# Two-layer hybrid diffusion block on one Trainium2 core: turned queries written into the free half of their own tile, neighbourhood queries staged two to a tile, squares of four heads in one instruction, and another order of VectorE and TensorE where each norm begins

## The chip, the cores and the metric

The kernel runs on one core of a Trainium2 chip. The metric is the device time of one execution, in microseconds (us), on that core; lower is better. The times of the kernel before are the median and the spread of three runs. One more execution was recorded by the hardware profiler; all durations below come from it.

## The reference, cut to what matters

256 latent tokens of width 2048, with 256 context tokens beside them in layer 0, pass through two layers. Layer 0 mixes with eight heads of a bidirectional gated DeltaNet and eight heads of neighbourhood attention; layer 1 mixes with a short gated convolution. Each layer ends with a SwiGLU network of 5632 hidden units. Everything is float32.

```python
for l in range(DEPTH):                                   # DEPTH = 2
    sh1, sc1, g1, sh2, sc2, g2 = split(silu(c) @ ada_w[l] + ada_b[l], 6)
    h = modulate(x_lat, norm_mix[l], sh1, sc1)           # rmsnorm * gain * (1 + sc) + sh
    y = even_mixer(h, hc, ...) if l == 0 else shortconv_mixer(h, ...)
    x_lat = x_lat + g1 * y
    x_lat = x_lat + g2 * swiglu(modulate(x_lat, norm_ffn[l], sh2, sc2), ...)
return rmsnorm(x_lat, final_norm)

def even_mixer(h, hc, w_in, ...):
    ka, va, kb, vb, a, b, qa, qb, za = split_segments(h @ w_in, EVEN_SEGS)
    ka, va, qa = short_conv_silu([ka, va, qa], conv_w)   # 5 taps along the tokens
    k_l = axial_rope(l2norm(heads(ka)))                  # l2norm: x * rsqrt(sum(x*x) + eps)
    q_l = axial_rope(l2norm(heads(qa))) * HEAD_DIM ** -0.5
    o_l, _ = gdn_bidirectional(q_l, k_l, heads(va), ...) # solve, inverse, scan over chunks of 64
    y_na = neighbourhood_attention(heads(qb), heads(kb), heads(vb), ...)
    return concat(y_gdn, y_na) @ w_out
```

## The kernel before

**Products.** Each float32 operand is split into a high and a low part, and each product is made of three matmuls: high by high, high by low, low by high. A weight arrives as a block of 512 KB, `raw` (128 partitions x 1024 float32), which SP loads (`load_w`, L232); `split_w` makes `whi` on ScalarE (a copy to fp32r, L175) and `wlo` on VectorE (a subtraction, L246). A block is a step of a stream (of the two forms below) where the stream is 1024 columns wide, and two steps where it is 512 wide.

**Streams.** `tm_stream` gives results with tokens on the partitions: per step, token tile (128 tokens, of which there are two) and block of 512 columns three matmuls, L299, L300 and L304. It keeps the last four steps for the end: there it takes block by block, each with four steps of three matmuls (L316), and after a block's twelve matmuls calls its evacuation. `fm_stream` gives results with features on the partitions, three matmuls (L342) per step and group of 128 features, and calls its evacuation for each group of 128 features on the last step. `grouped` collects the steps; behind a norm, the first HEAD = 4 steps are also done together, token tile by token tile. `Pump` runs the jobs of the conditioning product (`ada_w`, `araw`) between the steps.

**The end of a stream that a norm follows.** Three streams have such an end, each of two blocks on two token tiles: the mixer's output product (`ev_w_out`) ahead of layer 0's FFN, that FFN's down product ahead of the odd mixer, and the odd mixer's output (`od_w_out`) ahead of layer 1's FFN. `resid_evac` multiplies a block by the gate row (L1299), adds it to `xs`, the residual (L1300), and takes the sum of squares (L1301, ScalarE). After the first token tile's last block, `Lead.scale` makes the norm's factor of that tile and multiplies the first 512 columns by it (L1317). `Lead.turn` puts the four transposes (L194) of these 512 columns into TensorE's order, between the matmuls of the second tile's last block. `Norm.step` then takes a piece of 512 columns of one token tile: scale and shift from PSUM to `modt` (L1363, ScalarE), the cast to the high part (L1365 for the first piece, four casts of 128 columns, so that the first matmul can start early; L1367 for later ones), and the low part (L1368). `w_steps` makes the splits of the steps HEAD and HEAD + 1 (the fifth and sixth) of the next stream follow the last `modt` and the last `xc` (L1353) of the second tile's first piece; this pair of instructions is `Norm.behind`.

**The mixer.** Its stream of input products runs beside the DeltaNet chain: solves by DMA over DRAM (`zsol`, `lsol`, `dz`, `xd`), inverses, scans. Where each piece of that chain is placed between the stream's matmuls is a plan of step numbers (`P_INV = (30, 32, 82, 84)` for the inverses); within that the scheduler of the tile framework, which simulates the engines' times, sets the order of each engine, and of SP's DMA queue. A change of one instruction's cost or buffer can so change the order of all that follows.

- `head_evac` (L661) takes keys, values and queries of four heads. Four copies to `hst`, and then, deferred from step to step, `front` (`conv_silu`: the taps into a tile `cv`, of which there are CV = 4) and `back` (transposes into PSUM and a copy into `out_t`, a tile of 128 x 4 x 4 x 128: token tile, head, width). For keys (n = 4 token tiles) and queries (n = 2) the squares are summed on ScalarE, one instruction for each token tile and head (L687).
- `qa_evac` (L735) scales and rotates the queries in `qt` (that `out_t`; with n = 2 its last two of four quarters are empty), transposes two heads at a time, copies them to `qf` (another use of the four tiles `cv`) and sends them to DRAM with a DMA on SP (`qTd`).
- `stage` (L1170) copies the results of the neighbourhood attention's queries (256 columns, scaled), keys and values to a tile `nst` of 512 columns, of which there are three, and sends each with a DMA of its own on SP (`qb_d`, `kb_d`, `vb_d`, L1178).

The lines that matter most for the norm, as they stand before:

```python
                            if lead and ti and n == nb - 1 and g == 2:
                                before = lead.turn(ins)
...
                if not n:
                    DVE.tensor_copy(hi[:, k, tok], m[:, j, :])
            if n:
                DVE.tensor_copy(hi[:, ks_, tok], m)
            DVE.tensor_tensor(lo[:, ks_, tok], m, hi[:, ks_, tok], op=OP.subtract)
            if not n and t:
                self.behind = mi, xi
```

## Time and profile before

| what | value |
|---|---|
| median of three runs | 2759.35 us |
| the runs | 2752.03, 2759.35, 2764.47 us |
| the profiled execution | 2762.49 us |
| its span in the trace | 2760.7 us |
| busy: TensorE (PE) | 2663.2 us |
| busy: weight loads (PEld) | 2187.7 us |
| busy: VectorE (DVE) | 1908.4 us |
| busy: ScalarE (ACT) | 1284.3 us |
| mean granted clock of TensorE | 0.992 |
| weight splits on VectorE (L246), 800 | 969.0 us, 1221 ns each |
| weight copies on ScalarE (L175), 800 | 842.5 us, 1062 ns each |

The span is what the trace covers; the execution's own time has 1.8 us more around it. Busy times of different engines lie beside each other, so they don't add up to the span. TensorE's matmuls are pipelined: the length of one row of several is the time to the end of the last, and the pitch between two is less than the length of one. The granted clock is the share of full speed that the throttle gave TensorE. A row of the timeline has the start in us, the length in us, engine, line, operation and tiles, and in brackets the idle time of that engine just before it and who ended it.

### The profile page before, as it was taken

The numbers are of one execution on the slowest core, as the hardware profiler recorded it, in microseconds if no ns is written. First come the engines' busy times: TensorE is split into PE (matmuls) and PEld (weight loads), VectorE is DVE, ScalarE is ACT, GpSimd is POOL, SyncE is SP. The second block draws the span as 40 slices with busy tenths as digits, with TensorE's granted clock in tenths as the row PEclk, the third lists the DMA queues.
The fourth block names the chain that finished last, engine by engine and source line by source line (L and its number), as shares of the span: only waits on it lengthen the run. The fifth ranks groups of instructions, "written<-read, shape, count | busy, mean of one in ns | idle before, by whom it ended". The sixth has DMA issues, their size and how long they took to land.

```text
span 2760.7 us, 37649 instructions
## 1 busy us (share of the span) xinstructions
PE 2663.2 (96%) x13775; PEld 2187.7 (79%) x13775; DVE 1908.4 (69%) x2599; ACT 1284.3 (47%) x1923; POOL 52.5 (2%) x84
## 2 busy tenths in 40 slices
PE   5998999998989999999999999999999999999998
PEld 2588787886878788887888878887878888888886
DVE  2377787795768788777686668898678544445665
ACT  3267643333554544444455545444454444445554
POOL 0000000101000000000000000000000000000000
PEclk9999999999999999999999999999999999999999
DMA  9955478799747799998886548998569666656553
GB/s 345 329 180 162 138 240 286 230 316 285 227 182 263 264 335 328 352 324 309 276 297 193 194 148 323 321 329 290 190 230 334 222 195 186 190 186 222 192 193 114
DMA packets 287028, 684.81 MB, mean 248 GB/s; under 512 B 57209, under 2 KB 100833, under 8 KB 285307
## 3 DMA queue, kind: packets, MB, share of 16 engines
q1 hardware_dynamic: 280564, 669.26, 72.3%
q10 hardware_dynamic: 4375, 9.48, 1.0%
q0 software_dynamic: 1904, 3.67, 0.4%
q8 instruction: 108, 1.77, 0.2%
q14 instruction: 77, 0.63, 0.1%
HBM read 659.21 MB, written 23.10 MB: 247 GB/s over the span
## 4 chain that ended last, share of the span: by engine, by line
PE 74%; DMA 11%; DVE 7%; issue 3%; ACT 3%; SPq 2%; POOL 0%; DVEq 0%; ACTq 0%
PE mm L299 18%; PE mm L300 18%; PE mm L304 18%; PE mm L342 8%; DMA araw<-in_ada_w_dram 7%; PE mm L316 6%; DVE wlo L246 2%; PE sm L194 2%; DVE acc L396 2%; PE sm L574 1%; PE gd L342 1%; DVE acc L431 1%; DMA bq<-in_ev_rpb_dram 1%; DMA raw<-in_ev_w_in_dram 1%; ACT whi L175 1%
## 5 line engine op out<-in xcount | busy, mean ns | idle before, releaser
L246 DVE TENSOR_TENSOR wlo<-raw,whi 128x1024 fp32r<-128x1024 f32 x800 | 969.0, 1221 | 402.2 <-ACT whi L175 392.8
L175 ACT ACTIVATE whi<-raw 128x1024 fp32r<-128x1024 f32 x800 | 842.5, 1062 | 858.4 <-PE mm L304 618.5
L299 PE MATMUL mm<-whi,fhi 128*128 128x512 f32 x1232 | 484.5, 395 | 6.7 <-DVE fhi L1365 6.7
L300 PE MATMUL mm<-wlo,fhi 128*128 128x512 f32 x1232 | 481.7, 391 | 0.0
L304 PE MATMUL mm<-whi,flo 128*128 128x512 f32 x1232 | 389.9, 390 | 0.0
L396 DVE SCALAR_TENSOR_TENSOR acc<-araw,cT,acc 128x1024 f32<-128x1024 f32 x224 | 287.1, 1282 | 123.1 <-DMA araw<-in_ada_w_dram 116.2
L342 PE MATMUL mm<-hB,whi 128*128 128x512 f32 (+1 forms) x1064 | 276.9, 351 | 1.5 <-DVE hB L602 1.2
L299 PEld LDWEIGHTS mm<-whi,fhi 128*128 128x128 f32 x1232 | 232.5, 189 | 55.3 <-DVE fhi L1365 8.1
L300 PEld LDWEIGHTS mm<-wlo,fhi 128*128 128x128 f32 x1232 | 232.6, 189 | 47.0
L304 PEld LDWEIGHTS mm<-whi,flo 128*128 128x128 f32 x1232 | 231.1, 188 | 48.4
L299 PE MATMUL mm<-whi,ahi 128*128 128x512 f32 x664 | 259.0, 390 | 0.0
L300 PE MATMUL mm<-wlo,ahi 128*128 128x512 f32 x664 | 258.3, 389 | 0.0
L342 PEld LDWEIGHTS mm<-hB,whi 128*128 128x128 f32 x1064 | 183.5, 192 | 33.6 <-issue 4.2
L304 PE MATMUL mm<-whi,alo 128*128 128x512 f32 x664 | 206.7, 389 | 0.0
L342 PE MATMUL mm<-hB,wlo 128*128 128x512 f32 (+1 forms) x532 | 179.7, 351 | 0.0
L431 DVE SCALAR_TENSOR_TENSOR acc<-araw,cT,acc 128x512 f32<-128x512 f32 x192 | 142.6, 747 | 24.2 <-DMA araw<-in_ada_w_dram 19.9
L178 ACT ACTIVATE ahi<-prodT 128x256 fp32r<-128x256 f32 x176 | 73.0, 418 | 183.7 <-PE mm L300 182.3
L304 PEld LDWEIGHTS mm<-whi,alo 128*128 128x128 f32 x664 | 124.6, 188 | 25.9
L299 PEld LDWEIGHTS mm<-whi,ahi 128*128 128x128 f32 x664 | 124.6, 188 | 25.7
L300 PEld LDWEIGHTS mm<-wlo,ahi 128*128 128x128 f32 x664 | 124.7, 188 | 25.7
L299 PE MATMUL mm<-whi,dhi 128*128 128x512 f32 x336 | 132.3, 396 | 5.6 <-DVE dhi L1365 3.4
L300 PE MATMUL mm<-wlo,dhi 128*128 128x512 f32 x336 | 131.8, 393 | 0.0
(399 smaller groups left out, 3409.7 us busy)
## 6 DMA issues: line engine op xcount, KB each, us to landing
araw<-in_ada_w_dram SPq DMA_DIRECT2D x288, 512.0 KB
raw<-in_ffn_w_down_dram SPq DMA_DIRECT2D x176, 512.0 KB
raw<-in_ffn_w_gate_dram SPq DMA_DIRECT2D x160, 512.0 KB
raw<-in_ffn_w_up_dram SPq DMA_DIRECT2D x160, 512.0 KB
raw<-in_ev_w_in_dram SPq DMA_DIRECT2D x112, 512.0 KB
araw<-in_ada_w_dram SPq DMA_DIRECT2D x192, 256.0 KB
raw<-in_od_w_in_dram SPq DMA_DIRECT2D x96, 512.0 KB
raw<-in_ev_w_out_dram SPq DMA_DIRECT2D x32, 512.0 KB
```

What stands on the lines that cost most here:

```text
L175: ACT.activation(dst, src, AF.Copy)
L178: ACT.activation(hi, src, AF.Copy)
L194: return PE.transpose(dst, src, ident[:n, :n])
L246: last_lo[0] = DVE.tensor_tensor(lo, raw, hi, op=OP.subtract).ins
L299: PE.matmul(ps[ti][n], a, hi[:, n * 512:(n + 1) * 512], start=first, stop=False)
L300: ins = PE.matmul(ps[ti][n], a, lo[:, n * 512:(n + 1) * 512], start=False, stop=False).ins
L304: last_mm[0] = PE.matmul(ps[ti][n], b, hi[:, n * 512:(n + 1) * 512], start=False, stop=False).ins
L316: ins = PE.matmul(ps[ti][n], a(t), w[:, c_], start=False, stop=a is ll and hi is group[-1][0]).ins
L342: last_mm[0] = PE.matmul(o, wt, h_(slice(0, len(ws)), mv, k), start=i == 0 and g == 0 and j == 0, stop=i == len(ks) - 1 and g == len(group ...
L396: DVE.scalar_tensor_tensor(acc, raw, cT[:, k:k + 1], acc, op0=OP.mult, op1=OP.add)
L431: DVE.scalar_tensor_tensor(accs[n], raws.pop(i), cT[:, k:k + 1], accs[n], op0=OP.mult, op1=OP.add)
L574: PE.matmul(pr[32 * j:32 * j + 32, :], cT2[:, g + j, :], raw[:, j].rearrange("p s n -> p (s n)"), start=g == 0, stop=g == KT - 4)
```

## The change

It has five parts.

1. *Order at a norm.* `Lead.turn` puts its transposes behind the second of the four steps of the last block, no longer behind the third. `resid_evac` returns its first instruction on VectorE, the multiply by the gate row; that of the second tile's last block now comes after the casts of the first tile's first piece (a constraint on VectorE's order alone, not a wait). The split of step HEAD - 1 (the fourth) also follows `Norm.behind`, which is now a pair of the last `modt` and the last cast, and is set for the first tile's piece and again for the second's.
2. *Turned queries.* `qf` is no longer a tile of its own: it is the third or fourth quarter of `qt`.
3. *Neighbourhood queries.* `stage_pairs` puts two groups of 256 columns into one tile `nst` of 512, and one DMA sends both.
4. *Squares.* One ScalarE instruction squares the n x 128 columns of a head, and one VectorE reduction sums them, where n instructions did both; `sq` has two buffers of 512 columns.
5. `stage` loses two arguments that no caller needs any more.

```diff
@@ -252,7 +252,7 @@
         nk = 1024 // W
         for g in range(0, len(ks), nk):
             assert ks[g + nk - 1] == ks[g] + nk - 1
-            hi, lo = split_w(load_w(segs, ks[g], nk), behind.behind if behind and g // nk in (HEAD, HEAD + 1) else None)
+            hi, lo = split_w(load_w(segs, ks[g], nk), behind.behind if behind and g // nk in (HEAD - 1, HEAD, HEAD + 1) else None)
             for j in range(nk):
                 yield ks[g] + j, hi[:, j * W:(j + 1) * W], lo[:, j * W:(j + 1) * W]
 
@@ -261,7 +261,7 @@
     def follow(ins, before):
 
         tc.add_manual_dep(ins, before.name, mybir.DependencyInfo(mybir.DependencyClass.NoSync, mybir.DependencyReason.DATA),
-                          reason="TensorE's order")
+                          reason="the engine's order")
 
     def grouped(steps, n, head=1, tail=TAIL):
 
@@ -317,12 +317,14 @@
                                 if lead and before is not None:
                                     follow(ins, before)
                                 before = ins
-                            if lead and ti and n == nb - 1 and g == 2:
+                            if lead and ti and n == nb - 1 and g == 1:
                                 before = lead.turn(ins)
                         with Stack() as order:
                             if lead and ti:
                                 lead.first(order)
-                            evac(ti, n, ps[ti][n])
+                            done = evac(ti, n, ps[ti][n])
+                    if lead and ti:
+                        lead.last = done
                     if lead and not ti:
                         lead.scale()
             yield
@@ -682,9 +684,9 @@
                         tc.keep_in_program_order(ins)
                 acopy(out_t[:, 0:n, i, :], pt[:, 0:n * 128].rearrange("p (t e) -> p t e", t=n))
                 if sums:
-                    sq = kvp.tile([128, 128], F32, name="sq", tag="sq", bufs=1)
-                    for t in range(n):
-                        ACT.activation(sq, out_t[:, t, i, :], AF.Square, accum_out=ss[:, t, i:i + 1])
+                    sq = kvp.tile([128, 4, 128], F32, name="sq", tag="sq", bufs=2)[:, 0:n]
+                    ACT.activation(sq, out_t[:, 0:n, i, :], AF.Square)
+                    DVE.tensor_reduce(ss[:, 0:n, i], sq, axis=AX.X, op=OP.add)
 
 
             for g_, i in ((front, 0), (front, 1), (front, 2), (back, 0), (front, 3), (back, 1), (None, 0), (back, 2), (back, 3)):
@@ -738,7 +740,7 @@
             DVE.tensor_scalar(rq, rq, scale, None, op0=OP.mult)
             normalise(qt, 2, rq)
             for g in range(2):
-                qf = kvp.tile([128, 2, 256], F32, name="qf", tag="cv", bufs=CV)
+                qf = qt[:, 2 + g].rearrange("p h e -> p (h e)").rearrange("p (i e) -> p i e", i=2)
                 pt = smt()
                 for i in range(2):
                     for t in range(2):
@@ -1167,23 +1169,32 @@
     vb_d = dram.tile([128, 4, 1024], F32, name="vb_d")
     qb_d = dram.tile([128, 8, 256], F32, name="qb_d")
 
-    def stage(dst, n, by=None):
+    def stage(dst):
 
         def f(i, *p):
-            st_ = nsp.tile([128, 512], F32, name="nst", tag="nst", bufs=NST)[:, 0:n]
-            if by is None:
-                copy(st_, p[-1][:, 0:n])
-            else:
-                ACT.activation(st_, p[-1][:, 0:n], AF.Copy, scale=by)
+            st_ = nsp.tile([128, 512], F32, name="nst", tag="nst", bufs=NST)
+            copy(st_, p[-1])
             SP.dma_start(dst(i), st_)
         return f
 
+    def stage_pairs(dst):
+
+        held = []
+
+        def f(i, p):
+            if not held:
+                held.append(nsp.tile([128, 512], F32, name="nst", tag="nst", bufs=NST).rearrange("p (f t) -> p f t", f=2))
+            ACT.activation(held[0][:, i % 2, :], p[:, 0:256], AF.Copy, scale=scale)
+            if i % 2:
+                SP.dma_start(dst(i - 1), held.pop())
+        return f
+
     for q in range(2):
-        drive(fm_stream([(wv, C_QB + q * 512, 512)], ks, [0], stage(lambda f: qb_d[:, q * 4 + f, :], 256, scale)), pump, R_QB, counts=True)
+        drive(fm_stream([(wv, C_QB + q * 512, 512)], ks, [0], stage_pairs(lambda f: qb_d[:, q * 4 + f:q * 4 + f + 2, :])), pump, R_QB, counts=True)
     for q in range(2):
-        drive(fm_stream([(wv, C_KB + q * 512, 512)], ks, [0, 1], stage(lambda f: kb_d[:, q * 4 + f, :], 512)), pump, R_KB, counts=True)
+        drive(fm_stream([(wv, C_KB + q * 512, 512)], ks, [0, 1], stage(lambda f: kb_d[:, q * 4 + f, :])), pump, R_KB, counts=True)
         drive(tm_stream([(wv, C_VB + q * 512, 512)], ks, lhsh, [0, 1, 2, 3],
-                        stage(lambda t: vb_d[:, t, q * 512:(q + 1) * 512], 512)), pump, R_KB, counts=True)
+                        stage(lambda t: vb_d[:, t, q * 512:(q + 1) * 512])), pump, R_KB, counts=True)
     lga.close()
     yp = pool("y", stack=lgs, side="right")
 
@@ -1296,11 +1307,12 @@
             col = slice(c0 + n * 512, c0 + (n + 1) * 512)
             v = xs[:, ti, col]
             tmp = rpool.tile([128, 512], F32, name="rtmp", tag="rtmp", bufs=2)
-            DVE.tensor_tensor(tmp, p, row[:, col], op=OP.mult)
+            begun = DVE.tensor_tensor(tmp, p, row[:, col], op=OP.mult)
             DVE.tensor_tensor(v, tmp, v, op=OP.add)
             ACT.activation(jk, v, AF.Square, accum_out=ssx[:, ti, col.start // 512:col.start // 512 + 1])
             if gain is not None:
                 DVE.tensor_tensor(v, v, gain[:, col], op=OP.mult)
+            return begun.ins
         return f
 
     def norm_row(t):
@@ -1350,7 +1362,7 @@
                 if not n:
                     self.r[t] = norm_row(t)
                 xt_ = self.pool.tile([128, 512], F32, name="xc", tag="xc", bufs=4)
-                xi = DVE.tensor_scalar(xt_, xs[:, t, n * 512:(n + 1) * 512], self.r[t], None, op0=OP.mult)
+                DVE.tensor_scalar(xt_, xs[:, t, n * 512:(n + 1) * 512], self.r[t], None, op0=OP.mult)
                 p = smt()
                 for j in range(4):
                     ins = transpose(p[:, j * 128:(j + 1) * 128], xt_[:, j * 128:(j + 1) * 128]).ins
@@ -1362,12 +1374,14 @@
                 q = p[:, j * 128:(j + 1) * 128]
                 mi = ACT.activation(m[:, j, :], q, AF.Identity, bias=sh_[:, k:k + 1], scale=sc_[:, k:k + 1])
                 if not n:
-                    DVE.tensor_copy(hi[:, k, tok], m[:, j, :])
-            if n:
+                    xi = DVE.tensor_copy(hi[:, k, tok], m[:, j, :])
+            if not n and not t:
+                follow(self.lead.last, xi.ins)
+            if not n:
+                self.behind = mi, xi
+            else:
                 DVE.tensor_copy(hi[:, ks_, tok], m)
             DVE.tensor_tensor(lo[:, ks_, tok], m, hi[:, ks_, tok], op=OP.subtract)
-            if not n and t:
-                self.behind = mi, xi
 
         def rest(self, after):
             while self.todo:
@@ -1410,7 +1424,7 @@
         def g(*a):
             if not f:
                 f.append(resid_evac(row[0], c0))
-            f[0](*a)
+            return f[0](*a)
         return g
 
     for i in range(10):
```

What stands in the engines' order before and after is shown at three places. The rows hold line, operation and tiles, and how often a row repeats; line numbers after the change are higher by 10 to 16 at these places.

**VectorE, end of the mixer's output product and start of the norm ahead of layer 0's FFN**, from the scaling of the first tile's first piece. `rtmp<-mm,row` is the gate multiply of the second tile's two blocks, `wlo` are splits of the next stream, `fhi<-modt` the casts of the first tile. Before:

```order
L1317 TENSOR_SCALAR rtmp<-xs,nx0r 128x512
L1299 TENSOR_TENSOR rtmp<-mm,row 128x512
L246 TENSOR_TENSOR wlo<-raw,whi 128x1024
L1300 TENSOR_TENSOR xs<-rtmp,xs 128x512
L246 TENSOR_TENSOR wlo<-raw,whi 128x1024
L1299 TENSOR_TENSOR rtmp<-mm,row 128x512
L1365 CAST fhi<-modt 128x128 x4
L1300 TENSOR_TENSOR xs<-rtmp,xs 128x512
L1368 TENSOR_TENSOR flo<-modt,fhi 128x4x128
```

After:

```order
L1329 TENSOR_SCALAR rtmp<-xs,nx0r 128x512
L1310 TENSOR_TENSOR rtmp<-mm,row 128x512
L246 TENSOR_TENSOR wlo<-raw,whi 128x1024
L1311 TENSOR_TENSOR xs<-rtmp,xs 128x512
L1377 CAST fhi<-modt 128x128 x4
L1310 TENSOR_TENSOR rtmp<-mm,row 128x512
L1384 TENSOR_TENSOR flo<-modt,fhi 128x4x128
L1311 TENSOR_TENSOR xs<-rtmp,xs 128x512
L246 TENSOR_TENSOR wlo<-raw,whi 128x1024
L1320 TENSOR_REDUCE ss_7646<-ssx 128x1
```

The casts have moved ahead of one split and one multiply; that split now stands behind the second tile's last addition, just ahead of the reduction that begins the second tile's factor. On TensorE the four transposes `sm<-cs,rtmp` stand behind six matmuls of the last block instead of nine; all 24 matmuls of the first tile's head still stand ahead of the second tile's transposes.

**ScalarE, the same place**, from the square root of the first tile's factor (L219) to that of the second's. `jk,ssx<-xs` are the second tile's sums of squares. Before:

```order
L219 ACTIVATE nx0s<-nx0v 128x1
L175 ACTIVATE whi<-raw 128x1024 x2
L1363 ACTIVATE modt<-sm,sh_83,sc_84 128x128 x4
L1301 ACTIVATE jk,ssx<-xs 128x512 x2
L219 ACTIVATE nx1s<-nx1v 128x1
```

After:

```order
L219 ACTIVATE nx0s<-nx0v 128x1
L175 ACTIVATE whi<-raw 128x1024
L1375 ACTIVATE modt<-sm,sh_83,sc_84 128x128 x4
L175 ACTIVATE whi<-raw 128x1024
L1312 ACTIVATE jk,ssx<-xs 128x512 x2
L219 ACTIVATE nx1s<-nx1v 128x1
```

One of two weight copies has moved behind the scale and shift of the first piece.

**SP's DMA queue, where the neighbourhood queries of the first four heads are staged.** `raw` are the stream's weights, `araw` those of the conditioning product, `dz` the transfers at the end of the first solve. Before:

```order
L1178 DMA qb_d<-nst 128x256 x3
L232 DMA raw<-in_ev_w_in_dram 128x2x512
L426 DMA araw<-in_ada_w_dram 128x512 x5
L969 DMA dz<-zsol 8x8x1024 x2
L969 DMA dz<-lsol 8x8x1024 x2
L1178 DMA qb_d<-nst 128x256
```

After:

```order
L1189 DMA qb_d<-nst 128x512 x2
L232 DMA raw<-in_ev_w_in_dram 128x2x512
L428 DMA araw<-in_ada_w_dram 128x512 x5
L232 DMA raw<-in_ev_w_in_dram 128x2x512 x2
L428 DMA araw<-in_ada_w_dram 128x512
L232 DMA raw<-in_ev_w_in_dram 128x2x512
L428 DMA araw<-in_ada_w_dram 128x512 x2
L232 DMA raw<-in_ev_w_in_dram 128x2x512
L428 DMA araw<-in_ada_w_dram 128x512
L971 DMA dz<-zsol 8x8x1024 x2
L971 DMA dz<-lsol 8x8x1024 x2
```

Two transfers of pairs have taken the place of four, and the `dz` transfers have moved behind four more weight loads.

## The prediction, made before the changed kernel had run

> **What bounds the kernel now.** I read the page first for the busy shares, then the list of who waited for whom on TensorE, then the timeline around its longest pauses. The page and one row of a table of 50 us stretches (columns: length, then busy time and instruction count of PE, PEld, DVE, ACT and POOL, then granted clock, DMA share, GB/s):
>
> ```profile
> PE 2663.2 (96%) x13775; PEld 2187.7 (79%) x13775; DVE 1908.4 (69%) x2599; ACT 1284.3 (47%) x1923; POOL 52.5 (2%) x84
> ...
> 200.00:250.00 50.00, 46.07 (x375) 45.47 (x374) 36.67 (x86) 40.88 (x99) 3.26 (x8) 0.97 0.53 168
> ```
>
> TensorE works for 96% of the span of 2760.7 us, so only about 97 us are idle on it, and what the change can give is a part of those pauses and of what follows them. In the stretch from 200 to 250 us ScalarE is busy 40.9 of 50 us, more than VectorE, and TensorE pauses for 4 us: ScalarE is the helper that is short there. The list of waits (total us, times, longest):
>
> ```profile
> PE sm L194 <- ACT cv L658: 7.8, 3, 4.3
> PE mm L299 <- DVE fhi L1365: 6.7, 4, 2.5
> PE mm L342 <- ACT nst L1177: 6.2, 3, 2.8
> PE gd L1016 <- DMA xd<-dz: 3.6, 2, 2.7
> PE mm L299 <- DVE dhi L1365: 3.4, 2, 2.5
> PE mm L342 <- DVE hst L172: 3.0, 1, 3.0
> ```
>
> Rows two and five are the three norms: 6.7 + 3.4 = 10.1 us. The first, third and last lie in the mixer before 430 us, and the change touches the source of each. Around the first norm the timeline reads (start, length, engine, line, what; in brackets the idle time before it and who ended it):
>
> ```profile
> 894.05 2.01 ACT L175 ACTIVATE whi<-raw 128x1024 fp32r<-128x1024 f32 x2 [0.55 <-PE mm L316]
> 894.31 0.49 DVE L1317 TENSOR_SCALAR rtmp<-xs,nx0r 128x512 f32<-128x512 f32 x1
> 895.21 0.60 PE L194 MATMUL sm<-cs,rtmp 128*128 128x128 f32 x4
> 895.32 1.22 DVE L246 TENSOR_TENSOR wlo<-raw,whi 128x1024 fp32r<-128x1024 f32 x1
> 895.96 1.49 ACT L1363 ACTIVATE modt<-sm,sh,sc 128x128 f32<-128x128 f32 x4
> 896.12 0.40 PE L316 MATMUL mm<-whi,ylo 128*128 128x512 f32 x1
> 896.45 0.69 DVE L1300 TENSOR_TENSOR xs<-rtmp,xs 128x512 f32<-128x512 f32 x1
> 898.18 0.68 DVE L1299 TENSOR_TENSOR rtmp<-mm,row 128x512 f32<-128x512 f32 x1
> 898.79 0.62 DVE L1365 CAST fhi<-modt 128x128 fp32r<-128x128 f32 x4
> 899.06 0.50 PE L299 MATMUL mm<-whi,fhi 128*128 128x512 f32 x1 [2.54 <-DVE fhi L1365]
> 900.55 0.63 PE L299 MATMUL mm<-whi,fhi 128*128 128x512 f32 x1
> 900.86 0.16 DVE L1308 TENSOR_REDUCE ss<-ssx 128x1 f32<-128x4 f32 x1 [0.25 <-ACT jk L1301]
> 902.26 0.49 DVE L1353 TENSOR_SCALAR xc<-xs,nx1r 128x512 f32<-128x512 f32 x1
> 904.42 1.98 PE L304 MATMUL mm<-whi,flo 128*128 128x512 f32 x8
> 906.23 0.60 PE L194 MATMUL sm<-cs,xc 128*128 128x128 f32 x4
> 907.64 0.50 PE L299 MATMUL mm<-whi,fhi 128*128 128x512 f32 x1 [0.81 <-DVE fhi L1365]
> ...
> 900.00:902.50 2.50, 2.50 (x7) 1.91 (x7) 1.81 (x9) 0.93 (x3) 0.00 (x0) 0.50 0.54 193
> ...
> 1262.99 0.44 PE L194 MATMUL sm<-cs,sg 128*128 128x128 f32 x2 [2.49 <-DVE sg L1449]
> 1263.51 0.39 PE L300 MATMUL mm<-wlo,fhi 128*128 128x512 f32 x1
> ```
>
> TensorE ends the last stream at 896.5 and waits 2.54 us for the first of four casts (L1365) at 898.79, which on VectorE stand behind a weight split and the second token tile's multiply (L1299). Then the matmuls take 0.63 us instead of 0.40 (the 896.12 row), and the window row has the granted clock at 0.50. The first 16 matmuls take 904.42 - 899.06 = 5.36 us; at the pitch of the L304 row, (1.98 - 0.39) / 7 = 0.227 us, they would take 3.63. So half clock costs 1.7 us after the pause. The waits of the other two norms are as long (6.7 for two, 3.4 for one), and I take them as alike. The last two rows, of a later stage, serve rival C.
>
> **The norms, three times.** *Transposes one step earlier.* They stood after nine of the block's twelve matmuls, at 895.21; after six that is 895.21 - 3 x 0.227 = 894.53. But their input is ready at 894.31 + 0.49 = 894.80, and some 0.1 us pass before TensorE starts (the first cast is over at about 898.94, the matmul starts at 899.06). So they start at 894.9, TensorE loses 0.4 us, and its last slot ends at about 896.7 instead of 896.35. *ScalarE.* One whi stays ahead of the four modt (2.01 / 2, over at 895.1), the second goes behind them: modt from 895.5 to 897.0. *VectorE.* Up to the L1300 at 896.45 nothing moves. Then the casts stand next, at 897.05 (the pitch of such rows is 0.6, 898.18 to 898.79). The first matmul follows 0.27 us after the first cast, as now: 897.32 instead of 899.06. The pause shrinks from 2.7 to 0.6 us, and I take the half clock after it as gone.
>
> *What is late next.* Behind the casts stand L1299, the L1368 subtraction and L1300 at a pitch of 0.6, to 899.5, the fourth step's split of 1.22, to 900.6, and only then the reduction at 900.86, so the second tile's chain is no later than now. From there to the first xc are 1.40 us and 0.49 more for it: 902.5. TensorE needs the fourth step's low part after 14 matmuls, at 900.5, and loses about 0.2 us. Its 24 matmuls take 5.45 us, to 903.0, and the second tile's transposes start then instead of at 906.23. From there to the first matmul behind them stay 1.41 us, with the 0.81 us wait. The gain is **3.2 us a norm, 9.7 in all**: 1.74 from the casts, 1.7 from the clock, less 0.2 for the split. If the split takes longer than its cover and half of the clock's part stays, it is 1.7 a norm; nothing could bring more than 3.5. The splits that now also wait for the last cast are needed 5 us later.
>
> The next two parts rest on these rows of the mixer, from the timeline, and on windows of 2.5 to 3 us around three of its pauses (columns as before):
>
> ```profile
> 326.88 0.72 ACT L653 ACTIVATE cv<-hst,evcT 128x512 f32<-128x512 f32 x1 [7.95 <-DMA qTd<-qf]
> 329.60 1.12 PE L194 MATMUL sm<-cs,cv 128*128 128x128 f32 x4 [4.29 <-ACT cv L658]
> 330.00:332.50 2.50, 2.50 (x10) 2.01 (x9) 2.31 (x6) 2.10 (x4) 0.00 (x0) 0.50 0.09 36
> ...
> 398.44 0.38 ACT L1177 ACTIVATE nst<-mm 128x256 f32<-128x256 f32 x1 [8.58 <-DMA qb_d<-nst]
> 398.88 0.51 PE L342 MATMUL mm<-hA,whi 128*128 128x256 f32 x2 [2.78 <-ACT nst L1177]
> ...
> 428.51 1.22 PE L342 MATMUL mm<-hA,whi 128*128 128x512 f32 x2 [1.97 <-ACT nst L1177]
> 429.00:431.50 2.50, 2.50 (x7) 1.92 (x7) 0.00 (x0) 0.85 (x3) 0.00 (x0) 0.50 0.93 288
> ...
> 241.00:244.00 3.00, 3.00 (x16) 3.00 (x16) 2.60 (x6) 2.95 (x9) 0.00 (x0) 0.50 0.37 104
> ```
>
> **Turned queries in their own tile.** The tag cv has four buffers, and the turned queries hold two until their DMA has left, which in SP's queue stands behind eight lsol loads. ScalarE waited 7.95 us at 326.88, TensorE 4.29 at 329.60, and half clock follows. In the tile's free half nothing of this waits; the tile itself is next used by values a stream of 16 steps later. I take 4.3 + 1.7 = **6.0 us** (bounds 0 and 6.0: at the most the values' taps on VectorE, queued there too, end the wait in its place).
>
> **Queries staged in pairs.** Three staging buffers hold three evacuations of 256 columns, and the fourth waits for a DMA: ScalarE 8.58 us, TensorE 2.78 and 1.97, with half clock at 429. Pairs need two buffers per group of four, and four DMAs of twice the size take the place of eight. Gone: 4.75 us, and up to 1.7 of clock. Late next are the weights, whose loads wait in the same SP queue behind the rest, so I take **4** (bounds 0 and 6.4).
>
> ```profile
> L687 ACT ACTIVATE sq<-hq 128x128 f32<-128x128 f32 x48 | 14.7, 306 | 0.7
> L687 ACT ACTIVATION_READ_ACCUMULATOR sq<-hq 128x1 f32 x48 | 9.1, 190 | 0.0
> ...
> L1301 ACT ACTIVATE jk<-xs 128x512 f32<-128x512 f32 x32 | 20.1, 629 | 49.0 <-DVE xs L1300 42.6 <-issue 4.1 <-DVE nx0v L218 2.3
> ...
> L1230 DVE TENSOR_REDUCE m<-sm 128x1 f32<-128x512 f32 x14 | 9.5, 683 | 5.3 <-PE sm L1226 5.3
> ```
>
> **Squares.** 48 squares with their accumulator reads are 14.7 + 9.1 = 23.8 us of ScalarE. In their place stand 8 of 512 columns at 0.63 (the jk row) and 8 of 256 at 0.38 (the 398.44 row, same width): 8.1. VectorE gets 16 sums, between 8 x 0.68 and 16 x 0.68 (the TENSOR_REDUCE row reads 512 columns), 5.5 to 11 us; 13 of 50 us are idle on it there. ScalarE's lateness made the other waits for cv (7.8 - 4.3 = 3.5), those for hst (3.0) and the half clock at 241 (1.7). I take **5** of these 8.2 (bounds 0 and 8.2).
>
> **A new order.** The scheduler orders the mixer anew from 170 us on. Its other waits, of which that of the second solve, xd<-dz (3.6), is the longest that it can touch, may shrink or grow. I charge **4 us** (bounds -4 and +15, the latter below).
>
> Sum: -9.7 - 6.0 - 4 - 5 + 4 = -20.7. The profiled execution took 2762.5 us, 3.1 above the median of the three runs (0.1%, less than they spread). **2762.5 - 20.7 = 2742 us.**
>
> **Rivals.** *A: the mixer gives everything back.* If the chain of solve, inverse and scan sets its end, a stream that runs ahead only waits longer for it. For this speaks the wait for xd<-dz; against it that nearly all waits of the stream lie before this chain's first result. Then the norms alone count: 2753.
>
> *B: slower than before.* In SP's order the dz stores, the end of the first solve, now stand behind five weight loads instead of one. One load feeds 24 matmuls, of 128x256 in this stream:
>
> ```profile
> 201.88 1.12 PE L342 MATMUL mm<-hB,whi 128*128 128x256 f32 x8
> ```
>
> At (1.12 - 0.28) / 7 = 0.12 us that is 4 x 24 x 0.12 = 11.5 us. If the stream gains nothing before, the chain is 11.5 us late from there to the mixer's end, in pauses with two more half clocks: 14.9 - 9.7 = 5.2 more, 2768. It decides once the stream's gain before 400 us is under 2 us. Against it stand the 4.29 and 3.0 us waits, whose causes are taken away.
>
> *C: the clock still falls at each norm.* A pause of 2.49 us, ended at 1262.99, left matmuls at 0.39 us (the 1263.51 row); so length alone doesn't settle it, and a shorter pause with two small stalls around it might still count as idle. Then 3 x 1.7 come back: 2747. The Trainium skill, "TensorE: Matmul & The Clock Gate", section "HAM oscillation", has as its abstract rule that only idle gaps above about 3.4 us throttle. By that rule the half clock behind 2.54 us isn't the pause's doing and stays, and the sum would be C's. The trace disagrees as far as one row can: a pause of 2.54 us is followed by a granted clock of 0.50. The page's Part 1 says that the window is free-running, which would allow both rows; the trace of before doesn't settle it.
>
> *D: nothing changes*, because other waits take each place at once: 2760. The casts' new place in VectorE's order speaks against it.
>
> **Chances.** Forecast 0.62, A 0.20, B 0.08, C 0.06, D 0.04. The forecast's own bounds are the terms': with each at its better end (norms 10.5, 6.0, 6.4, 8.2, and 4 from the new order) 35.1 less, 2727; with the squares and pairs at nothing 2751. The range of **2727 to 2760** takes in A, C and D and leaves out B and what the terms miss. 0.5%, about what a measurement of this kernel can tell from no change, is 13.8 us: below 2745.6 counts as faster. From the forecast 0.57 lies there and 0.03 of C: **0.60 faster**. Slower than 2773 is half of B: **0.04**. The rest is **0.36 the same**.
>
> **What would show it.** In the changed profile: waits for the casts near 2 us for each norm (0.6 + 0.8 each, 4 in all, against 10.1) and a clock of 1.00 behind each; no wait for qTd in ScalarE's rows, none for qb_d, no nst among TensorE's waits but the first of 1.45; the hst wait small. The forecast is wrong if the waits between 430 and 830 us grow by over 10 us, above all L1016 for xd<-dz, or if the casts still stand late.

## The result and the profile after

| | before | changed |
|---|---|---|
| median | 2759.5 us (12 runs, 2752.03 to 2771.96) | 2748.7 us (12 runs, 2742.16 to 2752.63) |
| ratio, 95% interval | 1 | 0.9957, 0.9942 to 0.9971 |
| profiled execution | 2762.49 us | 2752.63 us |

The change makes the kernel 10.8 us faster, 0.43%, clear of its interval though under the 0.5% that the chances were set by. The forecast was 2742 us, 17 less than the median of before, in a range of 2727 to 2760. One execution among the experiments below (norms alone, 4485.9 us at a mean granted clock of 0.559) is left out of its ratio. The two profiled executions differ by 9.9 us; that of the change is the slowest of its twelve runs. The page after begins:

```profile
span 2750.9 us, 37578 instructions
PE 2664.0 (97%) x13775; PEld 2189.8 (80%) x13775; DVE 1915.8 (70%) x2615; ACT 1275.6 (46%) x1842; POOL 53.3 (2%) x84
```

TensorE is as busy as before; what fell is idle time. The list of who waited for whom on TensorE (total us, times, longest), with the rows that answer to those of before and those that are new:

```profile
PE gd L1018 <- DMA xd<-dz: 9.4, 2, 5.7
...
PE mm L299 <- ACT whi L175: 3.5, 2, 2.9
PE gd L1076 <- DVE R L1059: 3.4, 2, 3.2
...
PE mm L299 <- DVE fhi L1377: 2.6, 4, 0.8
...
PE sm L194 <- ACT cv L660: 1.9, 1, 1.9
...
PE mm L344 <- ACT nst L1187: 1.4, 1, 1.4
...
PE mm L299 <- DVE dhi L1377: 1.2, 2, 0.8
```

The waits for the casts fell from 10.1 to 3.8 us, those for cv from 7.8 to 1.9, for nst from 6.2 to 1.4, and the one for hst (3.0) is gone: all as the change meant. But xd<-dz grew from 3.6 to 9.4, whi from 0.4 to 3.5 and R from 0.6 to 3.4.

**The norms.** The first norm after, in the timeline:

```profile
893.79 0.49 DVE L1329 TENSOR_SCALAR rtmp<-xs,nx0r 128x512 f32<-128x512 f32 x1
894.34 0.66 PE L194 MATMUL sm<-cs,rtmp 128*128 128x128 f32 x4 [0.17 <-DVE rtmp L1329]
895.93 0.69 DVE L1311 TENSOR_TENSOR xs<-rtmp,xs 128x512 f32<-128x512 f32 x1
896.53 0.63 DVE L1377 CAST fhi<-modt 128x128 fp32r<-128x128 f32 x4
896.80 0.50 PE L299 MATMUL mm<-whi,fhi 128*128 128x512 f32 x1 [0.42 <-DVE fhi L1377]
902.57 0.60 PE L194 MATMUL sm<-cs,xc 128*128 128x128 f32 x4
903.98 0.50 PE L299 MATMUL mm<-whi,fhi 128*128 128x512 f32 x1 [0.81 <-DVE fhi L1377]
...
2006.80 0.73 PE L300 MATMUL mm<-wlo,fhi 128*128 128x512 f32 x2 [0.51 <-DVE wlo L246]
...
897.00:899.50 2.50, 2.50 (x12) 2.05 (x12) 2.50 (x6) 1.54 (x4) 0.00 (x0) 1.00 0.72 210
```

The pause is 0.42 us instead of 2.54, and the window row behind it has a granted clock of 1.00. From the scaling (893.79) to the second tile's first matmul (903.98) pass 10.19 us, where before had 907.64 - 894.31 = 13.33. The same measure is 10.17 at the second norm (13.35 before) and 11.03 at the third (13.33), where the fourth step's split comes 0.51 us late: the 2006.80 row. Together 40.0 - 31.4 = **8.6 us**; 9.7 were forecast.

**The mixer.** I call mixer time what passes from TensorE's start on the first matmul that waits for hB (149.87 before, 150.73 after, both after 1.15 us of idle time) to the scaling at the first norm: 744.4 us before, 743.1 after. So 1.4 us came from there in these two executions, where 11 were forecast. TensorE's stretches of 40 to 60 us show where the rest went (columns: length, then busy time and instruction count of PE, PEld, DVE, ACT and POOL, then granted clock, DMA share, GB/s). The first three rows are before, the last three after:

```profile
600.00:640.00 40.00, 40.00 (x215) 34.38 (x214) 35.88 (x74) 10.88 (x20) 3.67 (x4) 1.00 0.87 282
640.00:700.00 60.00, 51.11 (x675) 39.06 (x674) 30.43 (x49) 21.38 (x37) 6.23 (x9) 0.91 0.93 264
700.00:750.00 50.00, 49.72 (x270) 40.66 (x269) 35.55 (x71) 25.92 (x55) 0.00 (x0) 1.00 0.74 238
...
600.00:640.00 40.00, 35.62 (x197) 30.56 (x195) 30.54 (x68) 11.12 (x21) 6.07 (x8) 0.98 0.85 248
640.00:700.00 60.00, 51.74 (x676) 39.65 (x677) 36.21 (x61) 23.45 (x44) 3.24 (x3) 0.85 0.93 272
700.00:750.00 50.00, 43.93 (x227) 36.54 (x226) 32.53 (x63) 27.85 (x53) 0.00 (x0) 0.90 0.67 201
```

4.4 us idle from 600 to 640 and 6.1 from 700 to 750 are new (before: none and 0.3), and the clock is lower in all three. Much of the stream's gain ahead of 430 us was waited off between 600 and 750. The rest went into longer matmuls in this execution. Over the whole mixer time TensorE's idle time fell from 37.0 to 31.8 us, but its busy time grew from 707.4 to 711.2, with the same 4803 instructions: the clock's records hold 23.9 us of half clock there before and 47.8 after.

### The profile page after: what moved, and what is told of

It reads as the page before. It is cut to its first block, busy times and chain, and to the rows that moved or that the text cites. A ratio compares the mean times of both kernels' runs of the same rounds, so it can differ in the third digit from the quotient of the medians.

```text
span 2750.9 us, 37578 instructions
## 1 busy us (share of the span) xinstructions
PE 2664.0 (97%) x13775; PEld 2189.8 (80%) x13775; DVE 1915.8 (70%) x2615; ACT 1275.6 (46%) x1842; POOL 53.3 (2%) x84
## 4 chain that ended last, share of the span: by engine, by line
PE 75%; DVE 9%; DMA 9%; issue 3%; SPq 2%; ACT 2%; POOL 0%; DVEq 0%; ACTq 0%
PE mm L299 18%; PE mm L304 18%; PE mm L300 18%; PE mm L344 7%; DMA araw<-in_ada_w_dram 6%; PE mm L316 6%; DVE wlo L246 2%; PE sm L194 2%; DVE acc L398 1%; PE sm L576 1%; DVE acc L433 1%; PE gd L344 1%; SPq L992 1%; DVE cv L658 1%; DVE zsol L964 1%
```

## The experiments

Each ratio is against runs of the kernel before on the same chip, taken with the kernel's own; the sets were taken on four chips, with 4 to 12 runs of each kernel unless said otherwise. Two orders of the mixer occur often, and executions of one order differ: the mixer time of before's order was 744.4, 746.7, 745.8 and 741.7 us in four profiles (mean 744.6), that of the change's order 743.1, 740.8, 738.6 and 739.3 (mean 740.4). So the mixer's share of the change is nearer 4 us than 1.4, and one profile says nothing on 2 us. By the means of these profiles the 4 us are all idle time (35.9 to 31.6 us); the busy time is the same (708.7 and 708.9), and half clock lasts 27.3 us in before's order and 38.4 in the change's.

### Norms alone, mixer alone

Only the edits of part 1, or only those of parts 2 to 4, on the kernel before.

> Before with part 1 alone (order at the three norms); the mixer as before. Theory (the norms bring all of the gain, the mixer gives its parts back): 9 to 10 us less than before, ratio 0.9965, as for the whole change within 2 us; waits for the casts 3.8 us in all against 10.1, and no granted clock of 0.50 behind any of the three norms. Rival (the mixer's parts bring half of the 10.8 us): 5 us less, ratio 0.998. In both the scaling of the first norm's first piece starts within 2 us of 894.3, as before.

> Before with parts 2, 3 and 4 (turned queries in their tile, staging in pairs, squares in one instruction), the norms as before. Theory: 0 to 2 us less than before, ratio 0.9995, though TensorE's waits before 430 us for cv, hst and nst fall from 17 to about 3 us; in their place stand waits for xd<-dz near 640 us of 9 us (3.6 before). Rival (half of the gain is the mixer's): 5 us less, ratio 0.998.

Norms alone: 0.9972 (0.9958 to 0.9986). Mixer alone: 0.9974 (0.9964 to 0.9985), 7 us, with a mixer time of 740.8 us. For the norms both the theory's 0.9965 and the rival's 0.998 lie inside the interval; for the mixer the rival's 0.998 does and the theory's 0.9995 doesn't, so the norms don't bring everything. Together they would be 15 us; the whole change has 11 to 12, which the intervals allow. The mixer-only run also shows the price of the clock by itself: its second norm has the long pause, but no half clock behind it.

```profile
1640.25 0.50 PE L299 MATMUL mm<-whi,dhi 128*128 128x512 f32 x1 [2.54 <-DVE dhi L1374]
1640.82 0.40 PE L299 MATMUL mm<-whi,dhi 128*128 128x512 f32 x1
...
1640.00:1643.00 3.00, 2.75 (x12) 2.27 (x13) 2.41 (x11) 0.93 (x3) 0.00 (x0) 1.00 0.78 253
```

It takes 11.74 us from the scaling to the second tile, the other two 13.33 and 13.36: half clock costs 1.6 us, as forecast (1.7).

### The inverses two and four steps later

```diff
-P_INV = (30, 32, 82, 84)
+P_INV = (30, 32, 84, 86)      # and (30, 32, 86, 88)
```

> The whole change, with the third and fourth entries of the plan of inverses at steps 84 and 86 instead of 82 and 84, so that two more steps of the stream (24 matmuls of 0.227 us, 5.45 us) stand ahead of the second solve's inverse. Theory A (the chain of solve, inverse and scan sets the mixer's end, whatever the stream does): the wait for xd<-dz falls, but waits later in the chain grow as much; within 1.5 us of the change, ratio 0.996. Theory B (the fixed step number of the plan makes the wait, and the chain itself has slack): xd<-dz 9.4 to about 4 us, 5 us less than the change, ratio 0.994.

> As the one before, but four steps later (86 and 88), 10.9 us of matmuls. Theory A: within 1.5 us of the change, ratio 0.996, or slower, as the chain starts up to 1 us later. Theory B: the wait for xd<-dz is gone (under 1 us) and with it part of the half clock at 639 to 652 us; 9 to 12 us less than the change, ratio 0.992.

0.9956 (0.9940 to 0.9971) and 0.9959 (0.9943 to 0.9976). This tells nothing on either theory: the order on every engine is the same as in the change, for these entries are no longer what places the inverse. The runs serve as two more executions of the change.

### Which part of the norm's order counts

> Part 1 alone, without its earlier transposes (they stay behind the third step of the last block). From the scaling of a norm's first piece to the first matmul behind the second token tile's transposes before has 13.33 us at the first norm, the change 10.19. Theory (the casts' place on VectorE is what counts, since the addition ahead of them ends at 897.1 in any case): 10.2 to 10.4 us, first pause of 0.4 to 0.8 us, no clock of 0.50 behind it. Rival (the earlier transposes bring a part): 10.8 us or more.

> Of part 1 only the casts ahead of the second tile's last multiply; the split of the fourth step stays ahead of the casts, the transposes stay where they were. The casts come one multiply earlier, 0.6 us. Theory: the pause is 1.9 us instead of 2.54. If half clock follows pauses by their length alone and 1.9 is still long enough, 12.7 us from the scaling to the second tile's first matmul (13.33 before) and a clock of 0.50 behind each; if 1.9 us is too short for it, 11.0 us and no half clock.

Without the earlier transposes the three norms take 10.17, 10.20 and 10.57 us: those transposes bring nothing, as the casts wait for the addition in either case. The pauses are 0.81 us, and the clock stays at 1.00. With the casts alone moved they take 12.76, 12.75 and 11.13, after pauses of 1.95 us; at the first:

```profile
897.20 0.50 PE L299 MATMUL mm<-whi,fhi 128*128 128x512 f32 x1 [1.95 <-DVE fhi L1368]
...
898.00 0.39 PE L300 MATMUL mm<-wlo,fhi 128*128 128x512 f32 x1
...
898.87 0.63 PE L299 MATMUL mm<-whi,fhi 128*128 128x512 f32 x1
...
899.00:901.50 2.50, 2.50 (x8) 1.93 (x7) 1.24 (x7) 0.93 (x3) 0.00 (x0) 0.50 0.48 177
```

Two of three pauses of 1.95 us were followed by half clock, the third wasn't, so length alone doesn't decide. Each of the two kernels was run once (2757.12 and 2753.59 us), so they show these rows and nothing on the time.

### More work for the stream, more work for the chain

```diff
+    # queries' streams, first matmul of each of eight groups, ten times more
+    PE.matmul(o, wt, h_(slice(0, len(ws)), mv, k), start=True, stop=True)
```

```diff
         DVE.tensor_copy(lsol, zsol.rearrange("p r c -> p c r"))
+        if solves:                      # the second solve
+            for _ in range(2):
+                POOL.tensor_copy(zsol, zsol)
+        solves.append(0)
```

> The whole change, and in the two streams of the neighbourhood attention's queries (350 to 420 us) the first matmul of each of eight groups is issued eleven times instead of once: 80 more matmuls of 128x256 at a pitch of 0.12 us, 9.6 us more TensorE work, same results; this spends the stream's lead. Theory A (the end of the chain of solve, inverse and scan sets the mixer's end, the stream's lead is worth nothing): within 2.5 us of the change, ratio 0.996 to 0.997. Theory B (TensorE's work sets it): 9.6 us more than the change, ratio 0.999 to 1.0.

> The whole change, and behind the second solve two copies of its result onto itself on GpSimd, which is idle there: no work for TensorE, VectorE or ScalarE, only D us more in the chain (D is the two copies in the trace, some 3 to 8 us). The stream's matmuls take the time in between. Theory A: the chain's last step and the mixer's end come D later, less the wait of up to 2 us that the context's scan makes anyway; D = 5 would give 0.997 to 0.998. Theory B: the stream's work covers D, within 1.5 us of the change.

Theory B fell with the first run, theory A with the second. With 9.6 us *more* TensorE work (the ten repeats last 1.36 us, at the pitch of 0.12 expected) the kernel isn't slower, and by the middle values it is 6 us faster than the change: 0.9935 (0.9918 to 0.9952, which overlaps the change's 0.9942 to 0.9971), mixer time 731.9. So the amount of TensorE's work doesn't set the end. And with the chain held up, its timeline reads:

```profile
622.09 1.90 POOL L970 COPY zsol<-zsol 128x1024 f32<-128x1024 f32 x1 [29.78 <-DVE lsol L967]
...
625.30 1.04 POOL L970 COPY zsol<-zsol 128x1024 f32<-128x1024 f32 x1
...
661.02 0.90 PE L1024 MATMUL gd<-xd,n 32*32 32x32 f32 x64
```

From the first copy to the end of the second pass 4.3 us, the second inverse, ahead of which the scheduler has put 12 us more of the stream, starts 19 us later than in the change (661.0 - 151.4 = 509.6 us into the mixer, against 490.6), and the kernel takes the same time: 0.9953 (0.9935 to 0.9971), mixer time 740.0. The second inverse has room; a chain that is late from there on isn't what the mixer waits for.

What the faster run has is an earlier *first* inverse: 254.4 us into the mixer, against 269.0. The first solve, on VectorE, ended at 233.7 instead of 242.1.

### VectorE's load in the first solve, and the queue behind it

> The whole change, and no jobs of the conditioning product in the two streams of the neighbourhood attention's queries (rate 0.6 to 0): 19 sums of 0.74 us, 14 us of VectorE, leave the end of the first solve and are done later, beside the output product; TensorE's work is the same. Theory C (the mixer is TensorE's work plus its idle time at the chain's joints, and that falls where the chain comes earlier against the stream, as it did with more work in the stream): the first inverse starts 5 to 10 us earlier, idle time after it falls from 22 to about 15 us, 5 to 8 us less than the change, ratio 0.993. Rival D (the run with more work won by an order that fell well, VectorE's load is no part of it): within 2 us of the change, ratio 0.996.

> The whole change, and the loads of the inverted diagonal blocks (xd and xdT from dz) are issued from GpSimd's queue, not from SP's, where they stand behind weight loads that wait for buffers: in the change 14 us pass between the last dz and the first xd on SP at the first solve, 7 at the second. Theory C: both inverses can start up to 8 us earlier; 3 to 6 us less than the change, ratio 0.994. Rival D: the loads are late because the DMA engines are busy at those places (0.9 and more of their time), so the queue is no part of it; within 2 us of the change.

Without the sums the first solve ends at 227.0 and the first inverse starts at 243.4, 26 us earlier than in the change; 0.9946 (0.9932 to 0.9959), mixer time 733.9. The direction is theory C's, the time only by its profile: the interval reaches the change's. Its mechanism isn't shown: TensorE's idle time behind the first inverse stayed (28.1 us in the change, 28.4 here), and what fell is the busy time (711.2 to 703.6), with 27.9 us of half clock instead of 47.8. A much earlier chain isn't worth its lead either, since TensorE then waits for other things: 7.7 us for the neighbourhood queries' load from qb_d, 4.2 for PT. Its first norm takes 12.75 us instead of 10.19, as half clock behind a 2.88 us wait for acc runs into it.

The diagonals from GpSimd are a miss: 1.011 (1.0076 to 1.0145). In its queue each load goes out 0.3 us after the one before has landed, and a load takes 2.2 to 7.3 us to land; the 16 go out from 403 to 460 us. Two that follow each other in some 2.6 us:

```profile
438.69 0.65 POOL L992 DMA_DIRECT2D xd<-dz  x1 [1.97 <-issue]
441.24 0.66 POOL L992 DMA_DIRECT2D xd<-dz  x1 [1.90 <-issue]
```

On SP the same 16 take 12 us. The Trainium skill, "DMA: Bandwidth & Descriptors", section "Anatomy of one DMA — SWDGE (gpsimd) path", gives about 2.0 us of fixed cost for each such DMA; this trace agrees in size, with 2.2 us at best for these 64 KB. The first load went out here as soon as dz had landed, 7.8 us after the start of the last two dz (395.20 to 402.99). On SP in the change the same takes 13.7 us, so SP's queue can have cost some 6 us at that place at the most.

### Part 3 undone, part 2 undone

> The whole change without part 3: the neighbourhood queries staged one by one, as before. The prediction's own term: 4 us of waits come back, 4 us more than the change, ratio 0.9972. Theory E (a stall of the stream ahead of the first inverse costs nothing; what costs is the order that the scheduler makes of the stream's lead): the order puts the inverses where before had them (305 and 136 us of stream matmuls still to come at the two, 286 and 127 in the change, 305 and 136 in the run with more work in the stream), so the waits for nst of about 6 us come back and the idle time after the first inverse falls by more, from 22 to 10 to 15 us; the mixer up to the first norm's scaling takes 732 to 738 us (740 in the change), ratio 0.993 to 0.995.

> The whole change without part 2: the turned queries in tiles cv of their own, as before. The inverses stand at the same places against the stream as in the change. The prediction's own term: 6 us more than the change, ratio 0.998. Theory E: the wait for cv at 330 us comes back (some 4 us), and the waits for xd<-dz near 640 us, 9 us in the change, fall by about as much; within 2 us of the change, ratio 0.996.

**Without pairs the kernel is 10 us faster than the change**, by the middle values: 0.9921 (0.9903 to 0.9939), against 0.9957 (0.9942 to 0.9971), two intervals that just fail to touch. Its waits for nst are back (5.2 us), its mixer time is 730.3. Theory E has the direction and said less (0.993 to 0.995). Without the turned queries in their tile it is 4 us slower than the change by the middle values: 0.9971 (0.9960 to 0.9981), mixer time 745.9. The two intervals overlap, so neither the prediction's 6 us nor theory E's 2 us is excluded. The waits for xd<-dz, which theory E saw fall, stayed (9.3 us). ScalarE's wait for qTd came back (5.2 us), but TensorE's waits for cv between 300 and 430 us are 1.2 us there, none in the change, and 4.3 in one row before.

VectorE's groups in the first solve, from its first product to the copy that ends it (columns: count, then busy us and mean ns, then idle before). Before, from 323.5 to 394.1 us:

```profile
L656 DVE SCALAR_TENSOR_TENSOR cv<-hst,evcT,cv 128x510 f32<-128x510 f32 (+1 forms) x28 | 19.8, 738 | 1.7 <-ACT cv L653 1.7
L246 DVE TENSOR_TENSOR wlo<-raw,whi 128x1024 fp32r<-128x1024 f32 x16 | 19.5, 1216 | 1.6 <-ACT whi L175 1.6
...
L431 DVE SCALAR_TENSOR_TENSOR acc<-araw,cT,acc 128x512 f32<-128x512 f32 x13 | 9.6, 742 | 0.0
```

The change, 326.9 to 392.9 us:

```profile
L246 DVE TENSOR_TENSOR wlo<-raw,whi 128x1024 fp32r<-128x1024 f32 x17 | 20.7, 1220 | 1.7 <-ACT whi L175 1.7
L433 DVE SCALAR_TENSOR_TENSOR acc<-araw,cT,acc 128x512 f32<-128x512 f32 x17 | 12.7, 745 | 0.4 <-DMA araw<-in_ada_w_dram 0.4
L658 DVE SCALAR_TENSOR_TENSOR cv<-hst,evcT,cv 128x508 f32<-128x508 f32 (+1 forms) x16 | 11.5, 742 | 0.0
```

Without pairs, 324.3 to 381.7 us:

```profile
L246 DVE TENSOR_TENSOR wlo<-raw,whi 128x1024 fp32r<-128x1024 f32 x13 | 15.8, 1217 | 0.5 <-ACT whi L175 0.5
L658 DVE SCALAR_TENSOR_TENSOR cv<-hst,evcT,cv 128x508 f32<-128x508 f32 (+1 forms) x16 | 11.5, 740 | 0.0
...
L433 DVE SCALAR_TENSOR_TENSOR acc<-araw,cT,acc 128x512 f32<-128x512 f32 x13 | 9.7, 742 | 0.0
```

The table adds the three groups and sets the solve beside them; the first inverse is the first matmul gd<-xd, counted from the mixer's start.

| kernel | other VectorE work in the solve | the solve | first inverse | mixer time | ratio |
|---|---|---|---|---|---|
| before | 48.9 us | 70.5 us | 266.5 | 744.4 | 1 |
| the change | 44.9 | 65.9 | 269.0 | 743.1 | 0.9957 |
| without turned queries in their tile | 60.2 | 78.5 | 271.7 | 745.9 | 0.9971 |
| more work for the stream | 36.7 | 58.9 | 254.4 | 731.9 | 0.9935 |
| no sums | 27.1 | 51.6 | 243.4 | 733.9 | 0.9946 |
| without pairs | 37.0 | 57.5 | 254.6 | 730.3 | 0.9921 |

The solve is 18 to 25 us plus whatever else VectorE does meanwhile. With the stalls of the queries' stream gone, more of it stands within the solve in VectorE's order: in the change four more splits and four more sums than without pairs, 4 x 1.22 + 4 x 0.745 = 7.9 us of VectorE. Then SP's queue adds its part; the last row of each list is the first inverse. The change:

```profile
395.17 2.24 SPq L971 DMA_DIRECT2D dz<-lsol  x2
...
399.18 1.40 SPq L232 DMA_DIRECT2D raw<-in_ev_w_in_dram  x2
...
405.20 0.35 SPq L1189 DMA_DIRECT2D qb_d<-nst  x1
...
408.18 0.38 SPq L232 DMA_DIRECT2D raw<-in_ev_w_in_dram  x1
408.87 0.99 SPq L992 DMA_DIRECT2D xdT<-dz  x2
...
419.71 0.24 PE L1018 MATMUL gd<-xd,n 32*32 32x32 f32 x2
```

and without pairs:

```profile
386.31 2.75 SPq L971 DMA_DIRECT2D dz<-lsol  x2
389.16 1.02 SPq L428 DMA_DIRECT2D araw<-in_ada_w_dram  x1
390.27 2.29 SPq L232 DMA_DIRECT2D raw<-in_ev_w_in_dram  x3
392.65 0.87 SPq L428 DMA_DIRECT2D araw<-in_ada_w_dram  x1
393.72 2.14 SPq L992 DMA_DIRECT2D xdT<-dz  x2
...
404.45 0.24 PE L1018 MATMUL gd<-xd,n 32*32 32x32 f32 x2
```

From the start of the last two dz to the first load of it pass 13.7 us in the change, with the next pairs of queries among what stands between, and 7.4 here. Together with the 7.9 us these are the 14 us by which the first inverse starts later in the change, for a stall of some 5 us that was saved. That passes on to the mixer's end: from the first inverse to the scaling 474.1 us pass in the change and 475.7 without pairs, although 20 us more of the stream's matmuls are still to come there (304 against 284, at 0.227 and 0.12 us each). In all but two of the profiles this stretch is 470 to 480 us (no sums 490.5, diagonals from GpSimd 498); what sets its length isn't shown.

## Why the prediction was right, and where it was wrong

The side and the range held. The time lies between the forecast (2742) and rival A (2753), and its 0.43% in the class within 0.5%, which had the smaller chance: a gain of 17 us on the median was forecast, and 10.8 were measured. That is 6.7 us from the forecast and 4.3 from rival A's number, and the range of 33 us is wide: it held although one term had the wrong sign. The prediction's own sign of being wrong, over 10 us more of waits between 430 and 830 us, came close: TensorE's idle time there grew from 17.7 to 26.5 us. Step by step:

- **Norms, 9.7 us forecast, 8.6 measured.** The mechanism is shown: casts at 896.53 (forecast 897.05), a pause of 0.42 (0.6), clock 1.00, second tile 3.1 and 3.2 us earlier at two norms. The size is off where "TensorE loses about 0.2 us" to the fourth step's split: nothing at the first norm, 0.51 us at the third. The earlier transposes, costed as the start of the chain, had no part in it. Rival C (half clock stays) didn't come in the change.
- **Turned queries, 6.0 forecast.** Undone, 4 us come back by the middle values, within the noise of both. They didn't do so by TensorE's wait of 4.3 us: only 1.2 us of waits for cv came back there. What the run shows instead is that without this part 32 taps stand in the first solve and with it 16, which is 11.5 us of VectorE, and that the first inverse starts 2.7 us later.
- **Pairs, 4 us forecast.** This step failed, in its sign. The waits went as forecast (6.2 to 1.4 us), yet with the rest of the change in place the part costs 10 us. The half clock at 429 us that it was to remove is still there (429.8 to 436.6). "Late next are the weights" looked at the stream; what came later was the first solve, by the stream's own splits and sums and by SP's queue.
- **A new order, 4 us charged.** The mixer's three gains added up to 15 and brought about 4 by the profiles' means, 7 by the runs of mixer alone; in the profiled pair TensorE's idle time fell from 17.3 to 3.8 us ahead of the first inverse and grew from 19.7 to 28.1 behind it. This is the term that was mis-sized: 8 to 11 us instead of 4. The three half clocks at 1.7 us that the gains counted are part of it: one of the three stretches is gone (329 us), two are not, and the mixer has more half clock than before, not less.
- **Squares, 5 us forecast:** not tried by itself, so its part is open. The wait for hst is gone; a wait for cv of 1.9 us and 3.4 us of half clock behind it remain (245.5 to 248.9).
- **Rivals A and B** each had a piece of it. A's picture, that a stream running ahead only waits longer later, is what the profile after shows, but its cause, a chain that sets the end, doesn't hold from the second solve on: 19 us of delay at the second inverse cost nothing. B's queue is there (13.7 us from dz to its loads, 6.3 more than without pairs), at a price covered by the rest.

What stays open: what sets the 470 to 480 us behind the first inverse, since neither 20 us of TensorE's work nor 19 us of delay at the second inverse changes them by as much; and why a first inverse 11 us earlier still (no sums) brings no more.

## What to carry to other kernels

A stall removed from a stream that feeds TensorE is not saved time until one has asked which other engine will now be asked for more, and what slow chain shares that engine: here 5 us of stalls gave VectorE 8 us more work inside a serial solve. Where a scheduler places the work, undo each part of a change in the presence of the others; here the change without one of its parts beats both kernels by the middle values (0.9921). And look whether a table entry still moves anything before reading a result from it: two of these runs were the same program.

## What the hardware showed

- **Half clock after short pauses.** Behind pauses of 2.54 us at the norms the clock fell to 0.50 in five of six cases (three before, two of three in mixer only), behind 1.95 us in two of three, behind 0.35 to 0.81 us in none of six (the change and its run without the earlier transposes). The clock's records show stretches of 3.4 us and multiples of it (6.8, 10.2, 13.7). The Trainium skill, "TensorE: Matmul & The Clock Gate", section "HAM oscillation", gives as its abstract rule "no PE-idle gaps >~3.4µs"; these rows show half clock behind shorter pauses, and the measurement decides.
- **GpSimd's queue** sent each of 16 loads of 64 KB only 0.3 us after the one before had landed: 57 us from the first to the last, where SP's queue takes 12, and a kernel 1.1% slower than before.
